# Retention queries and keys as a seven-product scheme per head, and a new order of the products around it

## Chip, cores and metric

The kernel runs on one core of one Trainium2 chip. The metric is the device time of one execution in microseconds (us). Three executions of the kernel before took 1118.16, 1119.35 and 1121.62 us; the median is 1119.35 us.

## The reference, cut to what matters

One layer of a decoder: a retention branch and a latent attention branch read the same normalised input, each is projected and gated, and an MLP and a gated embedding follow. The sequence has 512 tokens, the model 1024 channels. The change is in the retention branch, which has 4 heads with 256 channels for queries and keys and 512 for values:

```python
proj = h @ w_in                       # h: 512 x 1024, normalised
rq, rk, rv, rg, cq, ckv, krope, gr, gm = jnp.split(proj, offsets, axis=-1)
rq = rope(rq.reshape(B, S, RET_HEADS, RET_QK_DIM), pos)
rk = rope(rk.reshape(B, S, RET_HEADS, RET_QK_DIM), pos) * (RET_QK_DIM ** -0.5)
ro = retention(rq, rk, rv)            # scores q k^T with a decay, times v
ro = rms_norm(ro, ret_norm...)
a_ret = (ro * jax.nn.silu(rg)) @ w_br
...
def rope(x, pos):                     # x1, x2: the two halves of 256
    return jnp.concatenate([x1 * cos - x2 * sin, x2 * cos + x1 * sin], axis=-1)
```

## The kernel before, in words

Every large product is made with split operands: a float32 number is held as a high and a low part (tiles that end in h and l, weights `wh_` and `wl_`), and `mm3` issues three matmuls for one pair of 128-row tiles: low by high, high by low, high by high. A weight tile of 512 KB (128 x 1024) is loaded raw (`wr_`), ScalarE rounds it to `wh_` (line 260), and VectorE subtracts to get `wl_` (line 264, or line 266 where the sign is turned). There are 6 raw buffers and NW=3 buffers each for the high and low parts, which all weights use in turn.

The program is a list of steps, `step(key, function, ...)`. `run_steps` walks through it, splits the next step's weights AHEAD=1 step early, and starts the raw loads of weights with an "sw" key up to PREP=3 steps early. The final order of the instructions on each engine is set by the framework's scheduler from these steps; each engine then takes its own instructions strictly in that order.

**Products in seven.** The values `rv` and the gates `rg` of two heads at a time, and the MLP's `dn`, are already made by a scheme of seven products instead of eight (Strassen-Winograd): operands are sums and differences of blocks, seven block products are formed, and four output blocks are combined from them. `CHAIN` says which products share one set of PSUM sums: 1, 6, 5, 3 accumulate in set a, 7 and 4 in set c, 2 alone in b. In between, `seven_out` reads the running sums out. The x operands (`XS[p]`) are made by `x_operand`; the weight operands are made by the DMA: `prepare` loads a block by SyncE's queue and adds others to it in the same buffer by accumulating loads on GpSimd's queue (POOL). A new raw tile is loaded for products 1, 7, 2, 5 and 3; 7 and 5 get a further block added at once, and products 6 and 4 are made by adding one more block to the tile of 7, once that tile has been split for the product before. The products come in the order 1, 7, 2, 6, 4, 5, 3. One product of `rv` or `rg` is 24 matmuls of 128x512.

**Queries and keys.** Each head has four projections, `rq` and `rk` with n=0 and n=1 (`ret_qk`), each 8 x 3 = 24 matmuls of 128x512. VectorE multiplies the sums by cos and sin (lines 809, 810), combines the two halves (lines 815, 816) and splits the result into `rqx`, `rqy`, `rkx`, `rky` (lines 305, 306).

**The rest of a head.** `ret_scores` (sums `rs`), `ret_attend` (sums `ro`, result `o`), `ret_gated` (`o` times the gate, line 851), `ret_turned` (transposes `ot` on TensorE), `branch_r` (four steps of 24 matmuls, sums `br`). The step list interleaves these with projections of the next head, so that TensorE has other work while VectorE finishes. After the heads come three `gr` gate steps (n = 5, 6, 7), between them the last `ret_turned`, then the last branch steps. In the attention phase before, `scores(h, blocks)` (sums `sc`) and `head_factor` (which ends with a small matmul `pbk`) alternate, and `fill` places steps of the gate projection `gm` into gaps.

Of the kernel before, what the change touches and what calls it, by code (L numbers as in the profile page):

```python
# [51 lines left out]

C_ID, C_MASK, C_IND, C_INVR, C_INVM, C_SGN, C_N = 0, 128, 256, 260, 261, 262, 263

NDYN, NKEEP, NW, NRAW, NDRAW, AHEAD, PREP, EARLY, PAD = 45, 16, 3, 6, 4, 1, 3, 5, 104
GROUPS = DFF // 1024


# [8 lines left out]
def _rng(a, n):  # L67
    return np.arange(a, a + n)


def chunk_specs():

    spec = {}

    def add(key, name, rows, cols):
        spec[key] = (len(rows) // P * len(cols), lambda w: _tiles(w[name], rows, cols))

    half = ROPE // 2
    cat = np.concatenate
    kr = cat([_rng(O_KR, half), _rng(O_KR + half, half), _rng(O_KR + half, half), _rng(O_KR, half)])  # L80
    first = cat([_rng(O_CKV, KVL), kr])
    full = _rng(0, D)
    for k in range(8):
        add(("a1", k), "w_in", _rng(k * P, P), first)
    for n in range(3):
        add(("cq", n), "w_in", full, _rng(O_CQ + n * P, P))
    for h in range(MH):
        spec["kq", h] = (2 * P + 3 * P, lambda w, h=h: cat([
            _tiles(w["w_ukv"], _rng(0, KVL), _rng(h * 256, P)), _tiles(w["w_uq"], _rng(0, QL), _rng(h * QKD, P))], axis=1))
    for p in range(4):  # L90
        add(("v", p), "w_ukv", _rng(0, KVL), cat([_rng(h * 256 + P, P) for h in (2 * p, 2 * p + 1)]))
    for gq in range(2):
        ac = cat([_rng((4 * gq + i) * QKD + NOPE, half) for i in range(4)])
        add(("qr", gq), "w_uq", _rng(0, QL), cat([ac, ac + half]))
    for n in range(8):
        for k in range(2):
            add(("gm", n, k), "w_in", _rng(k * S, S), _rng(O_GM + n * P, P))
            if n < EARLY:
                add(("gr", n, k), "w_in", _rng(k * S, S), _rng(O_GR + n * P, P))
        if n >= EARLY:  # L100
            add(("gr", n), "w_in", full, _rng(O_GR + n * P, P))
        for key, name in (("bm", "w_bm"), ("o", "w_o"), ("pg", "w_ple_gate")):
            add((key, n), name, full, _rng(n * P, P))
    for h in range(RH):
        for key, o in (("rq", O_RQ), ("rk", O_RK)):
            for n in range(2):
                add((key, h, n), "w_in", full, _rng(o + h * RQK + n * P, P))
        for k in range(4):
            add(("br", h, k), "w_br", _rng(h * RV, RV), _rng(2 * k * P, 2 * P))

    for kb in range(2):
        for fb in range(2):
            for q in range(RH // 2):
                for c in range(2):
# [32 lines left out]
def trunk_layer(ctx: ExitStack, tc: tile.TileContext, xT, pT, pos, gains, const, decay, wstream, outT):  # L147
# [314 lines left out]


    def trig(name, posf, inv):
        ang, kf, c_, s_ = T(name + "a"), T(name + "k"), T(name + "c"), T(name + "s")
# [686 lines left out]
    for h in range(MH):  # L1152
        p, more = h // 2, h + 2 < MH
        if h % 2 == 0 and h:
            step(None, scores, h, (0, 1))
            step(None, head_factor, h)
            step(None, scores, h, (2, 3))
            step(None, head_factor, h + 1)
        else:
            step(None, scores, h)  # L1160
# [49 lines left out]
            step(None, x_operand, 7)  # L1210
    for p in (1, 2, 4):
        step(None, x_operand, p)
    def qk(h, key, n):
        step((key, h, n), ret_qk, h, key, n)

    def branch(h, *ks):
        for k in ks if h >= 0 else ():
            step(("br", h, k), branch_r, h, k)

    for q in range(RH // 2):  # L1220
        h = 2 * q
# [8 lines left out]
        for kind in ("rv", "rg"):  # L1230
            for p in (1, 7, 2, 6, 4, 5, 3):
                for c in range(2):
                    step(("sw", (kind, q), p, c), ret_seven, kind, q, p, c)
                if (kind, q) == ("rv", 0) and p in (1, 7, 2):
                    step(None, x_operand, {1: 6, 7: 5, 2: 3}[p])
                if (kind, p) == ("rv", 1):
                    branch(h - 1, 2)
                    step(None, ret_scores, h)
                    branch(h - 1, 3)
                if (kind, p) == ("rg", 1):  # L1240
                    step(None, ret_attend, h)
                if (kind, p) == ("rg", 4):
                    step(None, ret_gated, h)
        qk(h + 1, "rq", 0)
# [132 lines left out]
```

## Time and profile before

| What | Value |
|---|---|
| median of 3 executions | 1119.35 us |
| the profiled execution, its own time | 1118.9 us |
| its span | 1117.1 us |
| TensorE (PE) busy | 1098.4 us, 98%, 5137 matmuls |
| weight loads (PEld) | 909.6 us, beside PE |
| VectorE (DVE) busy | 711.4 us, 64% |
| ScalarE (ACT) busy | 541.1 us, 48% |
| GpSimd (POOL) busy | 90.4 us, 8% |
| DMA | 178.02 MB; mean 159 GB/s |

A busy share is an average over the whole span. The releaser behind an arrow ("<-DVE wl_rg L266") is the instruction whose end let the waiting one start. Matmuls are pipelined: their shown durations overlap, so the cost of one is read from the distance between two starts.

### The profile page before, as it was taken

Reading aid. Unit: us, or ns where it says so; the run is one execution under the profiler, and the core shown is the slowest. Engines: PE = TensorE matmul, PEld = TensorE weight load, DVE = VectorE, ACT = ScalarE, POOL = GpSimd, SP = SyncE. Lnnn points to the kernel's source line nnn. Section 1 sums busy time; section 2 is a strip of 40 time slices with the busy share of each in tenths; the row PEclk is TensorE's granted clock in tenths of the full one; section 3 lists DMA queues with packets and bytes.
Section 4 is the critical chain, followed back from the end, with each engine's and each line's share of the span. In section 5 each row is a group of like instructions: output and inputs, shape, how many; then the busy total and the mean of one; then the engine's idle time right before and its main releaser. Section 6 shows DMA issues by size and latency. Waiting matters only on the chain.

```text
span 1117.1 us, 13841 instructions
## 1 busy us (share of the span) xinstructions
PE 1098.4 (98%) x5137; PEld 909.6 (81%) x5137; DVE 711.4 (64%) x1135; ACT 541.1 (48%) x785; POOL 90.4 (8%) x121
## 2 busy tenths in 40 slices
PE   9999999999999999999999999999999999999998
PEld 7877878888878788887878877788888888888887
DVE  7697677566774655646456467555466666668785
ACT  7637556453465635345554644434444443444552
POOL 0000000001102001031100100010100100101000
PEclk9999999999999999999999999999999999999999
DMA  7242231466779734488873934693855765737511
GB/s 263 63 136 76 64 104 57 141 208 220 185 189 241 196 124 169 108 195 209 205 212 96 281 121 145 197 265 116 178 161 166 177 168 152 185 129 195 163 57 57
DMA packets 59860, 178.02 MB, mean 159 GB/s; under 512 B 7376, under 2 KB 8784, under 8 KB 59536
## 3 DMA queue, kind: packets, MB, share of 16 engines
q1 hardware_dynamic: 45168, 129.66, 35.1%
q0 software_dynamic: 14480, 47.46, 21.7%
q8 instruction: 40, 0.66, 0.2%
q14 instruction: 28, 0.23, 0.1%
q10 hardware_dynamic: 144, 0.03, 0.0%
HBM read 157.97 MB, written 17.04 MB: 157 GB/s over the span
## 4 chain that ended last, share of the span: by engine, by line
PE 75%; DMA 9%; DVE 6%; issue 5%; ACT 2%; POOL 1%; SPq 0%; POOLq 0%; ACTq 0%; DVEq 0%
PE up L167 16%; PE dn L167 14%; PE br L167 5%; DMA wr_rg<-wstream 5%; PE pg L167 4%; PE bm L167 4%; PE wo L167 4%; PE gr L167 3%; PE rq L167 3%; PE rk L167 3%; PE gm L167 3%; PE rg L167 2%; DMA wr_rv<-wstream 2%; PE sc L167 2%; PE rv L167 2%
## 5 line engine op out<-in xcount | busy, mean ns | idle before, releaser
L167 PE MATMUL dn<-wh_dn,cl 128*128 128x512 f32 x224 | 87.2, 389 | 0.0
L167 PE MATMUL dn<-wh_dn,ch 128*128 128x512 f32 x224 | 87.1, 389 | 0.0
L167 PE MATMUL dn<-wl_dn,ch 128*128 128x512 f32 x224 | 87.1, 389 | 0.0
L260 ACT ACTIVATE wh_dn<-wr_dn 128x1024 fp32r<-128x1024 f32 x32 | 34.0, 1062 | 74.5 <-PE up L167 54.3
L260 ACT ACTIVATE wh_up<-wr_up 128x1024 fp32r<-128x1024 f32 x32 | 34.0, 1061 | 58.8 <-PE up L167 29.3
L264 DVE TENSOR_TENSOR wl_dn<-wr_dn,wh_dn 128x1024 fp32r<-128x1024 f32 x32 | 39.1, 1221 | 25.8 <-ACT wh_dn L260 25.8
L264 DVE TENSOR_TENSOR wl_up<-wr_up,wh_up 128x1024 fp32r<-128x1024 f32 x32 | 39.1, 1223 | 18.8 <-ACT wh_up L260 18.8
L167 PEld LDWEIGHTS dn<-wl_dn,ch 128*128 128x128 f32 x224 | 42.0, 188 | 8.8
L167 PEld LDWEIGHTS dn<-wh_dn,cl 128*128 128x128 f32 x224 | 42.0, 188 | 8.7
L167 PEld LDWEIGHTS dn<-wh_dn,ch 128*128 128x128 f32 x224 | 42.0, 188 | 8.6
L982 DVE SCALAR_TENSOR_TENSOR f<-up,bcx 128x512 f32<-128x512 f32 x32 | 20.6, 686 | 44.4 <-PE up L167 44.4
L260 ACT ACTIVATE wh_dn<-dr_dn 128x1024 fp32r<-128x1024 f32 x24 | 25.4, 1060 | 44.3 <-PE up L167 29.4
L264 DVE TENSOR_TENSOR wl_dn<-dr_dn,wh_dn 128x1024 fp32r<-128x1024 f32 x24 | 29.4, 1223 | 24.5 <-ACT wh_dn L260 24.5
L222 POOL DMA_DIRECT2D dr_dn<-wstream x24 | 21.1, 892 | 294.0 <-DVE wl_dn L264 107.5
L260 ACT ACTIVATE wh_rg<-wr_rg 128x1024 fp32r<-128x1024 f32 x28 | 29.4, 1059 | 30.6 <-DMA wr_rg<-wstream 15.5
L260 ACT ACTIVATE wh_rv<-wr_rv 128x1024 fp32r<-128x1024 f32 x28 | 29.4, 1059 | 29.7 <-DMA wr_rv<-wstream 7.2
L264 DVE TENSOR_TENSOR wl_rg<-wr_rg,wh_rg 128x1024 fp32r<-128x1024 f32 x20 | 24.3, 1224 | 20.6 <-ACT wh_rg L260 20.4
L264 DVE TENSOR_TENSOR wl_rv<-wr_rv,wh_rv 128x1024 fp32r<-128x1024 f32 x20 | 24.3, 1223 | 14.0 <-ACT wh_rv L260 14.0
L1040 DVE TENSOR_TENSOR d<-d,dn 128x1024 f32<-128x1024 f32 x24 | 29.3, 1219 | 6.0 <-PE dn L167 6.0
L264 DVE TENSOR_TENSOR wl_br<-wr_br,wh_br 128x1024 fp32r<-128x1024 f32 x16 | 19.5, 1220 | 21.2 <-ACT wh_br L260 21.2
L260 ACT ACTIVATE wh_br<-wr_br 128x1024 fp32r<-128x1024 f32 x16 | 16.9, 1059 | 31.7 <-PE rk L167 16.3
L871 ACT ACTIVATE rt<-br 128x512 f32<-128x512 f32 x24 | 13.9, 594 | 25.5 <-PE br L167 25.5
(1819 smaller groups left out, 3449.2 us busy)
## 6 DMA issues: line engine op xcount, KB each, us to landing
wr_up<-wstream SPq DMA_DIRECT2D x32, 512.0 KB, 4.1
wr_dn<-wstream SPq DMA_DIRECT2D x32, 512.0 KB, 3.5
dr_dn<-wstream POOLq DMA_DIRECT2D x24, 512.0 KB, 7.0
wr_rv<-wstream SPq DMA_DIRECT2D x20, 512.0 KB, 4.2
wr_rg<-wstream SPq DMA_DIRECT2D x20, 512.0 KB, 4.8
wr_rv<-wstream POOLq DMA_DIRECT2D x16, 512.0 KB, 7.1
wr_rg<-wstream POOLq DMA_DIRECT2D x16, 512.0 KB, 7.9
wr_br<-wstream SPq DMA_DIRECT2D x16, 512.0 KB, 3.6
```

Source lines behind the costliest of these rows:

```text
L167: return tc.keep_in_program_order(nc.tensor.matmul(*a, **k))
L222: nc.gpsimd.dma_start(raw, chunk(("w", blk, kb, fb, c)), accum_op=ALU.add)
L260: i = ACT(hi, raw, AF.Copy, scale=sign)
L264: TT(lo, raw, hi.bitcast(F32), op=ALU.subtract)
L871: ACT(t, ps, AF.Copy)
L982: STT(u[:, i], ps[:, i], 0.0, V["bcx2"], op0=ALU.max, op1=ALU.mult)
L1040: TT(to, to, dps[p], op=ALU.add if sign > 0 else ALU.subtract)
```

## The change

Each head's four projections become one product in seven. Queries are one output half and keys the other; with the input halves and the token halves this gives a two-by-two block form. One of its products has 4 x 2 x 3 = 24 matmuls of 128x256 (stationary: 128 columns of the weights; moving: 256 tokens of `XS[p]`, which the `rv` and `rg` products use too), so a head has 168 of them. The results come as blocks of 256 tokens; they are multiplied by a table `tab` (cos, sin, cos, with one more ScalarE copy) and combined in 256-column pieces. The keys are now "sw" keys, so their weights are loaded by `prepare`.

The order of all sevens changes from 1, 7, 2, 6, 4, 5, 3 to 1, 7, 2, 6, 5, 4, 3, so that product 4 (set c) stands between 5 and 3, which share set a. Products of a head's queries and keys are placed among others: those of head 0 between products of `rv`, products 1 and 7 of an odd head between `rg` 6 and 5, its product 2 after `rg` 3. Smaller moves: two `fill` steps of `gm` before `rotary_key` and one after (before: one and two), score blocks 0, 1, 2 ahead of `head_factor` (before: 0, 1), and the last `ret_turned` after the `gr` step 6 (before: after 5).

```diff
-NDYN, NKEEP, NW, NRAW, NDRAW, AHEAD, PREP, EARLY, PAD = 45, 16, 3, 6, 4, 1, 3, 5, 104
+NDYN, NKEEP, NW, NRAW, NDRAW, AHEAD, PREP, EARLY, PAD = 42, 16, 3, 6, 4, 1, 3, 5, 104
...
+            for h in range(RH):
+                add(("w", ("qk", h), kb, fb, 0), "w_in", _rng(kb * S, S), _rng((O_RQ, O_RK)[fb] + h * RQK, RQK))
...
-    def ret_qk(w, h, key, n):
-        d = R[h]
-        ps = proj(B(f"{key}{h}{n}"), xn, w)
-        a, b = T(f"{key}a{h}{n}"), T(f"{key}b{h}{n}")
-        TT(a, ps, V["cr"] if n == 0 else V["sr"], op=ALU.mult)
-        TT(b, ps, V["sr"] if n == 0 else V["cr"], op=ALU.mult)
-        if n == 0:
-            d[key] = (a, b)
-        else:
-            a0, b0 = d[key]
-            TT(a0, a0, a, op=ALU.subtract)
-            TT(b0, b0, b, op=ALU.add)
-            d[key] = (split(a0, f"{key}x{h}"), split(b0, f"{key}y{h}"))
+    def ret_qk(w, h, p):
+        ch, d = CHAIN[p], R[h]
+        if p in (1, 7, 2):
+            qkps[ch] = B(f"qk{h}{p}")
+        ps = qkps[ch]
+        for o in range(2):
+            for k in range(4):
+                mm3(ps[:, o * 256:o * 256 + 256], cut(w, k * 256 + o * P), XS[p][k], p in (1, 7, 2) and o + k == 0,
+                    o == 1 and k == 3, skip_group_check=True)
+        done = seven_out(d.setdefault("qk", {}), p, ps, f"qk{h}_")
+        if not done:
+            return
+        blk, t = done
+        key, cs = ("rq", "rk")[blk % 10 - 1], slice(256 * (blk // 10 - 1), 256 * (blk // 10))
+        a, b = T(f"{key}a{h}{blk}"), T(f"{key}b{h}{blk}")
+        TT(two(a), two(t), V["tab"][:, 0:2, cs], op=ALU.mult)
+        TT(two(b), two(t), V["tab"][:, 1:3, cs], op=ALU.mult)
+        first = key not in d
+        if first:
+            d[key] = (T(f"{key}u{h}"), T(f"{key}v{h}"))
+        u, v = d[key]
+        TT(u[:, cs], a[:, 0:256], a[:, 256:512], op=ALU.subtract)
+        TT(v[:, cs], b[:, 0:256], b[:, 256:512], op=ALU.add)
+        if not first:
+            d[key] = (split(u, f"{key}x{h}"), split(v, f"{key}y{h}"))
...
+    fill(2)
+    step(None, rotary_key)
     fill(1)
-    step(None, rotary_key)
-    fill(2)
...
-            step(None, scores, h, (0, 1))
+            step(None, scores, h, (0, 1, 2))
             step(None, head_factor, h)
-            step(None, scores, h, (2, 3))
+            step(None, scores, h, (3,))
...
         if q:
+            qk(h, 1, 7, 2)
             step(None, ret_turned, h - 1)
-        qk(h, "rq", 1)
-        branch(h - 1, 0)
-        qk(h, "rk", 0)
-        branch(h - 1, 1)
-        qk(h, "rk", 1)
...
+            qk(h, 6)
+            branch(h - 1, 0)
+            qk(h, 5, 4, 3)
+            branch(h - 1, 1)
+            seven("rv", q, 1)
+            branch(h - 1, 2)
+            step(None, ret_scores, h)
+            seven("rv", q, 7, 2, 6)
+            branch(h - 1, 3)
+        else:
+            step(None, x_operand, 6)
+            qk(h, 1, 7)
+            step(None, x_operand, 5)
+            qk(h, 2)
+            seven("rv", q, 1)
+            step(None, x_operand, 3)
+            qk(h, 6)
+            seven("rv", q, 7)
+            qk(h, 5)
+            seven("rv", q, 2)
+            qk(h, 4, 3)
+            seven("rv", q, 6)
+            step(None, ret_scores, h)
+        seven("rv", q, 5, 4, 3)
+        seven("rg", q, 1)
+        step(None, ret_attend, h)
+        seven("rg", q, 7, 2, 6)
+        qk(h + 1, 1, 7)
+        seven("rg", q, 5, 4)
+        step(None, ret_gated, h)
+        seven("rg", q, 3)
+        qk(h + 1, 2)
         step(None, ret_turned, h)
+        qk(h + 1, 6)
         branch(h, 0)
+        qk(h + 1, 5, 4, 3)
         branch(h, 1)
         step(None, ret_scores, h + 1)
...
-        if n == EARLY:
+        if n == EARLY + 1:
             step(None, ret_turned, RH - 1)
```

How the rows move is shown at two places. In the rows, `<-` stands between what an instruction writes and what it reads; `rs` are the sums of the scores, `s` the scores times the decay.

**The scores of head 1, VectorE and ScalarE.** The scores' first matmul reads the low part `rkx1l`. Before, VectorE:

```order
L815 TENSOR_TENSOR rka_4019<-rka_4019,rka_4094 128x512
L816 TENSOR_TENSOR rkb_4020<-rkb_4020,rkb_4095 128x512
L264 TENSOR_TENSOR wl_br_3_4217<-wr_br_3_4214,wh_br_3_4216 128x1024
L306 TENSOR_TENSOR rkx1l<-rka_4019,rkx1h 128x512
L306 TENSOR_TENSOR rky1l<-rkb_4020,rky1h 128x512
L830 TENSOR_TENSOR s_4157<-rs_4150,dec_4148 128x512
L264 TENSOR_TENSOR wl_rq_0_4257<-wr_rq_0_4254,wh_rq_0_4256 128x1024
```

Of the change, VectorE and then ScalarE (`wr_qk_4432` is the weight tile of product 1 of head 2's queries and keys):

```order
L831 TENSOR_TENSOR rka_4306<-qk_3867,tab 128x512
L832 TENSOR_TENSOR rkb_4307<-qk_3867,tab 128x512
L837 TENSOR_TENSOR rku_4229<-rka_4306 128x256
L838 TENSOR_TENSOR rkv_4230<-rkb_4307 128x256
L265 SCALAR_TENSOR_TENSOR wl_qk_4472<-wr_qk_4432,wh_qk_4471 128x1024
L305 TENSOR_TENSOR rkx1l<-rku_4229,rkx1h 128x512
L305 TENSOR_TENSOR rky1l<-rkv_4230,rky1h 128x512
L853 TENSOR_TENSOR s_4369<-rs_4362,dec_4360 128x512
```

```order
L259 ACTIVATE wh_br_3_4428<-wr_br_3_4426 128x1024
L304 ACTIVATE rqx1h<-rqu_4080 128x512
L304 ACTIVATE rqy1h<-rqv_4081 128x512
L259 ACTIVATE wh_qk_4471<-wr_qk_4432 128x1024
L304 ACTIVATE rkx1h<-rku_4229 128x512
L304 ACTIVATE rky1h<-rkv_4230 128x512
```

The weights that the program needs next stood behind `rkx1h` and `rkx1l` before; in the change those of head 2's first product stand ahead of both. With three buffers, `wh_qk_4471` goes into the one of the second branch step's weights. At head 3 the rows are the same with the `gr` weights of n = 5 in that place.

**The scores of head 0, VectorE.** Before, where each `rk` projection's sums come 5 rows ahead of the next:

```order
L809 TENSOR_TENSOR rka_3119<-rk_3094,trs 128x512
L810 TENSOR_TENSOR rkb_3120<-rk_3094,trc 128x512
L815 TENSOR_TENSOR rka_3083<-rka_3083,rka_3119 128x512
L816 TENSOR_TENSOR rkb_3084<-rkb_3084,rkb_3120 128x512
L264 TENSOR_TENSOR wl_rv_3155<-wr_rv_3091,wh_rv_3154 128x1024
L306 TENSOR_TENSOR rkx0l<-rka_3083,rkx0h 128x512
```

Of the change, from behind the sum that product 4 completes (`qk_21_3191`, with a weight split after it):

```order
L831 TENSOR_TENSOR rqa_3350<-qk_21_3191,tab 128x512
L832 TENSOR_TENSOR rqb_3351<-qk_21_3191,tab 128x512
L837 TENSOR_TENSOR rqu_3100<-rqa_3350 128x256
L838 TENSOR_TENSOR rqv_3101<-rqb_3351 128x256
L263 TENSOR_TENSOR wl_rv_3429<-wr_rv_3368,wh_rv_3428 128x1024
L305 TENSOR_TENSOR rqx0l<-rqu_3100,rqx0h 128x512
L305 TENSOR_TENSOR rqy0l<-rqv_3101,rqy0h 128x512
L831 TENSOR_TENSOR rka_3395<-qk_2991,tab 128x512
L832 TENSOR_TENSOR rkb_3396<-qk_2991,tab 128x512
L837 TENSOR_TENSOR rku_3269<-rka_3395 128x256
L838 TENSOR_TENSOR rkv_3270<-rkb_3396 128x256
L263 TENSOR_TENSOR wl_rv_3496<-wr_rv_3413,wh_rv_3495 128x1024
```

Directly behind the last of them stands `rkx0l`, then the weights `wl_rv_3513` and `rky0l`. Queries and keys of the second token half are finished right before the scores, where before only the second half of the keys was.

## Rows read from the trace of the kernel before

**Rows 1.** The page: busy times; DMA queues (packets, MB, share of 16 engines).

```profile
PE 1098.4 (98%) x5137; PEld 909.6 (81%) x5137; DVE 711.4 (64%) x1135; ACT 541.1 (48%) x785; POOL 90.4 (8%) x121
...
q1 hardware_dynamic: 45168, 129.66, 35.1%
q0 software_dynamic: 14480, 47.46, 21.7%
```

**Rows 2.** Timeline, PE: first matmuls of rq and of rk (48 apart).

```profile
275.44 0.39 PE L167 MATMUL rq<-xn0h,wl_rq 128*128 128x512 f32 x1
286.32 0.39 PE L167 MATMUL rk<-xn0h,wl_rk 128*128 128x512 f32 x1
```

**Rows 3.** Timeline, PE: the same form with 256 columns (first and last of 41).

```profile
1107.56 0.28 PE L167 MATMUL pg<-x3g2l,wh_pg 128*128 128x256 f32 x1
...
1112.36 0.28 PE L167 MATMUL pg<-x3g7h,wh_pg 128*128 128x256 f32 x1
```

**Rows 4.** Groups by line, PE, 270 to 660 us: matmuls that waited (busy, mean ns | idle before).

```profile
L167 PE MATMUL rg<-wl_rg,xn4h 128*128 128x512 f32 x8 | 3.4, 419 | 0.9 <-DVE wl_rg L266 0.9
L167 PE MATMUL rv<-wh_rv,s30l 128*128 128x512 f32 x8 | 3.3, 414 | 0.9 <-DVE cv L754 0.9
L167 PE MATMUL rg<-wh_rg,s30l 128*128 128x512 f32 x8 | 3.3, 410 | 0.9 <-DVE z L754 0.9
...
L167 PE MATMUL rg<-wl_rg,xn6h 128*128 128x512 f32 x8 | 3.2, 404 | 0.8 <-DVE wl_rg L266 0.8
L167 PE MATMUL rv<-wl_rv,xn6h 128*128 128x512 f32 x8 | 3.2, 402 | 0.5 <-DVE wl_rv L266 0.5
```

**Rows 5.** Timeline, PE: the last transposes, and those of head 1.

```profile
641.75 0.39 PE L167 MATMUL gr<-xn7h,wh_gr 128*128 128x512 f32 x1
...
644.97 1.20 PE L167 MATMUL ot<-cst,o 128*128 128x128 f32 x9 [0.34 <-DVE o L851]
...
450.48 0.81 PE L167 MATMUL ot<-cst,o 128*128 128x128 f32 x3
451.62 0.55 PE L167 MATMUL ot<-cst,o 128*128 128x128 f32 x3 [0.33 <-DVE o L851]
```

**Rows 6.** Timeline, PE: two waits of the attention phase.

```profile
68.77 0.47 PE L167 MATMUL gm<-xg0h,wl_gm 128*128 128x512 f32 x1 [1.55 <-DVE wl_gm L264]
...
161.21 0.65 PE L167 MATMUL pbk<-cst,hr 128*128 128x128 f32 x4 [1.00 <-DVE hr L602]
```

**Rows 7.** Timeline around the scores of head 1: PE, DVE and ACT.

```profile
417.81 0.39 PE L167 MATMUL rk<-xn7h,wh_rk 128*128 128x512 f32 x1
418.23 0.69 DVE L809 TENSOR_TENSOR rka<-rk,trs 128x512 f32<-128x512 f32 x1 [2.63 <-PE rk L167]
418.84 0.68 DVE L810 TENSOR_TENSOR rkb<-rk,trc 128x512 f32<-128x512 f32 x1
420.64 1.22 DVE L264 TENSOR_TENSOR wl_br<-wr_br,wh_br 128x1024 fp32r<-128x1024 f32 x1
421.77 0.68 DVE L306 TENSOR_TENSOR rkx1l<-rka,rkx1h 128x512 fp32r<-128x512 f32 x1
...
418.23 1.06 ACT L260 ACTIVATE wh_br<-wr_br 128x1024 fp32r<-128x1024 f32 x1 [3.89 <-PE rk L167]
```

**Rows 8.** Timeline, DVE: four operations on 256 columns, one group.

```profile
311.93 1.43 DVE L733 TENSOR_TENSOR sy<-xr,xr 128x256 f32<-128x256 f32 x4
```

**Rows 9.** DMA issues, 270 to 650 us: KB each, median us to landing.

```profile
wr_rg<-wstream POOLq DMA_DIRECT2D x16, 512.0 KB, 7.9
```

**Rows 10.** Stretches: span, busy of PE, PEld, DVE, ACT, POOL, granted clock, DMA share, GB/s.

```profile
270.00:650.00 380.00, 373.58 (x1689) 307.20 (x1688) 222.39 (x325) 191.57 (x286) 52.40 (x67) 1.00 0.70 185
...
1112.00:1114.00 2.00, 0.64 (x6) 0.43 (x4) 0.84 (x2) 0.42 (x1) 0.00 (x0) 1.00 0.19 66
1114.00:1116.00 2.00, 0.00 (x0) 0.00 (x0) 0.43 (x2) 0.00 (x0) 0.00 (x0) 0.74 0.19 66
```

**Rows 11.** Timeline, PE: the first matmuls of the program.

```profile
1.46 4.21 PE L167 MATMUL zero<-zero 128*128 128x512 f32 x9 [1.46 <-DVE zero L360]
```

More of the change, by code (lines that the diff above doesn't have):

```diff
@@ L104, in chunk_specs @@
     for h in range(RH):
-        for key, o in (("rq", O_RQ), ("rk", O_RK)):
-            for n in range(2):
-                add((key, h, n), "w_in", full, _rng(o + h * RQK + n * P, P))
         for k in range(4):
@@ L464, in trig @@
     def trig(name, posf, inv):
-        ang, kf, c_, s_ = T(name + "a"), T(name + "k"), T(name + "c"), T(name + "s")
+        ang, kf = T(name + "a"), T(name + "k")
+        if name == "tr":
+            V["tab"] = dyn.tile([P, 3, S], F32, tag="tab", name="tab", bufs=1)
+            c_, s_ = V["tab"][:, 0], V["tab"][:, 1]
+        else:
+            c_, s_ = T(name + "c"), T(name + "s")
         TS(ang, posf, inv, None, op0=ALU.mult)
@@ L503, in ret_sincos @@
     def ret_sincos():
-        V["cr"], V["sr"] = sincos(*V["ar"])
+        sincos(*V["ar"])
+        ACT(V["tab"][:, 2], V["tab"][:, 0], AF.Copy)
     def rotary_key():
@@ L747, in seven_out @@
             to = {1: 11, 7: 22, 6: 21}[p]
-            c[to] = (T if to == 21 or name[0] == "c" else Z)(f"{name}{to}")
+            c[to] = (Z if to != 21 and name[0] == "z" else T)(f"{name}{to}")
             ACT(c[to], ps, AF.Copy, scale=1.0 if p == 7 else -1.0)
@@ L803, in odd_v, with two @@
             R[h]["v"][j] = split(src, f"rv{h}{j}", lo=lo)
-    def ret_qk(w, h, key, n):
-        d = R[h]
-        ps = proj(B(f"{key}{h}{n}"), xn, w)
-        a, b = T(f"{key}a{h}{n}"), T(f"{key}b{h}{n}")
-        TT(a, ps, V["cr"] if n == 0 else V["sr"], op=ALU.mult)
-        TT(b, ps, V["sr"] if n == 0 else V["cr"], op=ALU.mult)
-        if n == 0:
-            d[key] = (a, b)
-        else:
-            a0, b0 = d[key]
-            TT(a0, a0, a, op=ALU.subtract)
-            TT(b0, b0, b, op=ALU.add)
-            d[key] = (split(a0, f"{key}x{h}"), split(b0, f"{key}y{h}"))
+    qkps = {}
+    def two(t):
+        return t.rearrange("p (k c) -> p k c", k=2)
+    def ret_qk(w, h, p):
[23 more added lines that the diff above has]
+            d[key] = (split(u, f"{key}x{h}"), split(v, f"{key}y{h}"))
     def ret_scores(h):
@@ L1212, in trunk_layer, with qk, seven @@
         step(None, x_operand, p)
-    def qk(h, key, n):
-        step((key, h, n), ret_qk, h, key, n)
+    def qk(h, *ps):
+        for p in ps:
+            step(("sw", ("qk", h), p, 0), ret_qk, h, p)
+    def seven(kind, q, *ps):
+        for p in ps:
+            for c in range(2):
+                step(("sw", (kind, q), p, c), ret_seven, kind, q, p, c)
     def branch(h, *ks):
@@ L1221, in trunk_layer @@
         h = 2 * q
-        qk(h, "rq", 0)
         if q:
+            qk(h, 1, 7, 2)
             step(None, ret_turned, h - 1)
-        qk(h, "rq", 1)
-        branch(h - 1, 0)
-        qk(h, "rk", 0)
-        branch(h - 1, 1)
-        qk(h, "rk", 1)
[L1230 to L1244, printed above, removed]
+            qk(h, 6)
[7 more added lines that the diff above has]
+            branch(h - 1, 3)
+        else:
+            step(None, x_operand, 6)
[20 more added lines that the diff above has]
+        qk(h + 1, 2)
         step(None, ret_turned, h)
-        qk(h + 1, "rq", 1)
-        qk(h + 1, "rk", 0)
+        qk(h + 1, 6)
         branch(h, 0)
-        qk(h + 1, "rk", 1)
+        qk(h + 1, 5, 4, 3)
         branch(h, 1)
```

## The prediction, made before the changed kernel was run

> **What bounds the kernel now.** I read the page first: TensorE (PE) is busy 98% of the span, VectorE (DVE) 64%, ScalarE (ACT) 48% [rows 1]. So the time is the sum of the matmuls plus the pauses between them, and the change can pay in two ways only: fewer or cheaper matmuls, or fewer pauses. The timeline gives the price of a matmul from start to start, the groups by line show which matmuls waited and for whom, the stretches give clock and DMA load. In 270 to 650 us, where the change lies, PE has 373.58 us of work in 380.00 at a granted clock of 1.00, beside a DMA share of 0.70 [rows 10]. Idle DVE and ACT there are cover for what the change adds to them, as long as no matmul waits for its result.
>
> The sum is made against the profiled execution, 1118.9 us; the median of the runs shown is 1119.35 us, 0.45 us above it, far inside their spread. A measurement of this kernel can tell about 0.3% from no change, 3.4 us: below about 1116.0 is faster, above 1122.7 slower.
>
> **Fewer columns.** 48 matmuls of 512 columns take 286.32 - 275.44 = 10.88 us, 0.2267 us each [rows 2]; a head's 96 take 21.76 us. With 256 columns, 40 distances from 1107.56 to 1112.36 make 0.120 us each [rows 3]; a head's 168 take 20.16 us. Gain 1.60 us a head, **6.4 us** for four. The new form is that of rows 3 (128 weight columns stationary, 256 tokens moving), so I take its price as it is. One rule speaks against this: the Trainium skill ("TensorE: Matmul & The Clock Gate", section "Back-to-back issue gap") gives sustained 81 ns for 128 columns and 131 ns for 512; halfway in columns that makes, as my estimate from the page, 98 ns for 256, and by it a head would lose 168 x 98 - 96 x 131 ns = 3.9 us, the kernel 15.6. The trace agrees with neither figure: 226.7 ns for 512 and 120 ns for 256, and the measurement decides.
>
> **The new order of all sevens.** Product 4 waits for weights that are still being added up in the tile of 7, and product 3 for the read-out of set a behind product 5. Idle before them is 0.9 + 0.9 + 0.9 + 0.8 + 0.5 = 4.0 us [rows 4], nine waits by the timeline. A shown matmul lasts 0.39 us where the next would start after 0.23, so each wait costs 0.16 us more than its idle time: 4.0 + 1.4 = **5.4 us**. With 5 ahead of 4, 4 has 24 matmuls (5.44 us) more for waits of under 1 us, and with 4 ahead of 3, set a has 5.44 us to be read. I count all of it; the bounds are 0 and 5.4.
>
> **Smaller moves.** The last transposes: from 641.75 to 644.97 us where one matmul and three transposes (0.11 us each, nine in 1.20) would take 0.56, so 2.66 us [rows 5]; a `gr` step of 5.44 us is put in between, gain **2.7 us**. Head 1's transposes: 1.14 us instead of 0.33 [rows 5], now with product 6, 2 or later work ahead, **0.8 us**. `pbk` waits 1.00 us [rows 6] and gets one more score block ahead, **1.0 us**. The `gm` weights come 1.55 us late [rows 6]; in the new order one DVE operation of 0.6 us less stands ahead, **0.6 us**. Gains together 16.9 us. The table's extra copy and the new `fill` order lie beside PE work.
>
> **New waits.** The engines are in-order. A DVE operation costs from start to start 0.61 us on 512 columns, 1.13 on 1024 [rows 7], and (1.43 - 0.42) / 3 = 0.34 on 256 [rows 8]; it starts 0.19 us after the sums it needs (417.81 + 0.23 to 418.23), and ACT rounds a weight tile in 1.06 [rows 7].
> - Head 1's scores. ACT now has `wh_qk` of head 2 ahead of `rkx1h`, and DVE `wl_qk` ahead of `rkx1l`. The buffer of `wh_qk` is free only when the second branch step ends, and the scores follow that step directly. So PE stands: 0.19 + 1.06 + 0.08 + 1.13 + 0.69 and 0.1 to PE, **3.2 us**.
> - Head 3's scores: the same with the `gr` weights, **3.2 us**. Head 2's have a product of `rv` and a branch step between and are covered.
> - Head 0's scores. From the sum of product 4 to `rkx0l` DVE has eight operations on 512 columns, four on 256 and three on 1024: 4.9 + 1.4 + 3.4 = 9.7 us, with 0.19 of lag and an estimated operation left over (0.6) 10.5. PE has product 3 (2.88) and an `rv` product (5.44), 8.3. A wait of 2.1 us or a little more; then `wl_rv` and `rky0l` (1.73) against three matmuls (0.68), 1.0 more: **3.1 us**.
> - The first `rv` product's second half. Behind head 0's product 2 DVE has a sum, two splits and two multiplications (5 x 0.61), two pieces of 256 (0.68) and the weights (1.22), 5.1 us with lag, against 2.72 of PE work and 0.23: **2.2 us**.
>
> Together 11.7 us. Each lies between nothing (if DVE and ACT reach that place earlier than I assume) and its chain at full durations, some 10% more: 0 to 13 us.
>
> **DMA.** A head's four loads of 512 KB become five on SyncE's queue and four accumulating ones on POOL's. By the queues of rows 1 the first kind takes 35.1% of 1117.1 us x 0.524 / 129.66 = 1.6 us of all engines, the second 21.7% x 1117.1 x 0.524 / 47.46 = 2.7; so 12.3 us a head, 49 in all, and the share in the stage rises from 0.70 to some 0.83. Accumulating loads land in 7.9 us [rows 9]. The tightest users: product 4 of heads 1, 2, 3 starts 2.88 + 5.44 + 2.88 = 11.2 us after product 6, whose split frees the tile; 7.9 and a split of 2.3 make 10.2. Product 6 of head 2 is about as tight. Nothing in the trace shows this load; bounds are 0 and a wait like the worst of rows 4 (0.9 + 0.16) at all four, 4 us. I take **0.7 us**, since 1 us is left at the median landing.
>
> **Sum:** 1118.9 - 6.4 - 5.4 - 2.7 - 0.8 - 1.0 - 0.6 + 11.7 + 0.7 = **1114.4 us**.
>
> **Rivals.**
> - *The new waits are covered.* DVE and ACT are far from full, and three of the four waits rest on a few operations of backlog. Without any: 1114.4 - 11.7 = 1102.7 us; with half, 1108.5. Against it stands the in-order place of `wh_qk` and its buffer, which no faster engine moves. Chance 0.20.
> - *Accumulating loads come late: slower.* The four tight products wait once landings pass 8.9 us; at 12 us each waits some 3 us, 12 us in all: 1114.4 - 0.7 + 12 = 1125.7. It makes the kernel slower from about 2.2 us a product (4 x 2.2 = 8.8 against the 8.6 from 1114.4 - 0.7 up to 1122.3). For it: the higher share, and product 4's waits in rows 4. Against it: the median landing. Chance 0.12.
> - *The clock falls in the two pauses of 3.2 us.* At the end of the program, behind the last matmul at 1112.36 [rows 3], the granted clock is 1.00 up to 1114 and 0.74 in the next two us [rows 10]; at the start, at 1.2 GHz, nine matmuls took 4.21 us [rows 11] instead of 9 x 0.227 = 2.04. Twice 2.2 us gives 1118.8: no change. The Trainium skill (the same page, section "Why this matters for your kernels") warns of idle gaps between bursts of matmuls; pauses of up to 1.55 us here left the clock at 1.00 [rows 6, 10]. Chance 0.08.
> - *The new order doesn't do what it is for:* loads and read-outs are late by the same amount, since more traffic stands ahead. Without its 5.4 us: 1119.8, no change. Chance 0.06.
> - *Weight loads bound the 256-column matmuls.* They take 909.6 / 5137 = 0.177 us each [rows 1]; 168 x 0.177 = 29.7 us a head instead of 20.2 would make 1152.6. Rows 3 have as many loads per matmul and run at 0.120. Chance 0.02.
>
> **How the numbers follow.** My forecast has 0.52, its own range 1109.5 to 1118 by the bounds of the new waits and of the DMA: 0.40 of it faster, 0.12 within 0.3%. Faster: 0.40 + 0.20 = 0.60. The same: 0.12, the clock 0.07, the order 0.05, late loads 0.02, together 0.26. Slower: late loads 0.10, clock and order 0.01 each, weight loads 0.02, together 0.14. The range reaches to 1103.0, leaving out some 0.06 of the covered case, and to 1121.0, leaving out late and bound loads, some 0.12.
>
> **What would show it.** Starts of `qk` matmuls 0.120 us apart; no idle before products 4 and 3 of `rv` and `rg`, none over 0.3 us before the last `ot` or `pbk`; idle of about 3 us before the first `rs` matmul of heads 1 and 3, released by `rkx1l` and `rkx3l`, 2 to 3 before that of head 0, and 2 in the first `rv` product; none before head 2's. Idle before `qk` products 4 or 6 with a weight load behind it means late loads; a granted clock under 1.00 in the stretch of a pause means the clock. The prediction is wrong if `rs` starts without a wait, or if a pause stands at a place not named here.

## The result, and the profile after

The changed kernel took 1124.24 us (median of 9 executions, 1122.7 to 1125.97) beside 1119.35 us before: a ratio of 1.0042, 95% interval 1.0031 to 1.0053. By the ratio it is slower by 4.7 us, where 1114.4 was forecast with a range of 1103 to 1121. The profiled execution took 1124.27 us, its span is 1122.5.

The page's first part of the changed kernel (answers to [rows 1]):

```profile
PE 1096.4 (98%) x5425; PEld 925.9 (82%) x5425; DVE 734.4 (65%) x1175; ACT 562.7 (50%) x812; POOL 104.1 (9%) x137
```

PE has less work than before, 1096.4 against 1098.4 us, in a longer span. A matmul at half clock is shown longer (0.63 instead of 0.39 us, below), so part of the gain is hidden even in the busy time.

**What came as the prediction said.** The timeline, PE, the first matmuls of three `qk` products, 24 apart (answers to [rows 2, 3]):

```profile
281.10 0.28 PE L166 MATMUL qk<-xn0h,wl_qk 128*128 128x256 f32 x1
283.98 0.28 PE L166 MATMUL qk<-s70h,wl_qk 128*128 128x256 f32 x1
286.86 0.28 PE L166 MATMUL qk<-xn4h,wl_qk 128*128 128x256 f32 x1
```

2.88 us for 24, 0.120 us each. The groups by line, PE, 270 to 660 us (answers to [rows 4, 5]):

```profile
L166 PE MATMUL rv<-wl_rv,xn6h 128*128 128x512 f32 x8 | 3.1, 389 | 0.0
L166 PE MATMUL rv<-wh_rv,s30l 128*128 128x512 f32 x8 | 3.1, 389 | 0.0
...
L166 PE MATMUL rg<-wl_rg,xn4h 128*128 128x512 f32 x8 | 3.1, 389 | 0.0
...
L166 PE MATMUL rg<-wh_rg,s30l 128*128 128x512 f32 x8 | 3.1, 389 | 0.0
L166 PE MATMUL ot<-cst,o 128*128 128x128 f32 x64 | 7.6, 273 | 0.0
```

No product 4, no product 3 and no transpose waits any more in this stretch, and `pbk` no longer waits in the attention phase. The DMA share in 270 to 650 us rose from 0.70 to 0.82, where 0.83 was forecast. The new waits stand where they were forecast. The scores of head 1, from the timeline (answers to [rows 7]):

```profile
427.43 0.39 PE L166 MATMUL br<-rog03h,wh_br 128*128 128x512 f32 x1
427.90 1.06 ACT L259 ACTIVATE wh_qk<-wr_qk 128x1024 fp32r<-128x1024 f32 x1 [3.00 <-issue]
428.99 1.23 DVE L265 SCALAR_TENSOR_TENSOR wl_qk<-wr_qk,wh_qk 128x1024 fp32r<-128x1024 f32 x1 [0.73 <-ACT wh_qk L259]
430.13 0.69 DVE L305 TENSOR_TENSOR rkx1l<-rku,rkx1h 128x512 fp32r<-128x512 f32 x1
430.88 0.80 PE L166 MATMUL rs<-rqx1h,rkx1l 128*128 128x512 f32 x1 [3.06 <-DVE rkx1l L305]
431.47 0.63 PE L166 MATMUL rs<-rqx1l,rkx1h 128*128 128x512 f32 x1
431.90 0.63 PE L166 MATMUL rs<-rqx1h,rkx1h 128*128 128x512 f32 x1
```

The chain is the forecast one, step by step: the branch step ends, ACT rounds head 2's weights, DVE splits them, then comes `rkx1l`. From 427.43 to 430.88 are 3.45 us; less one matmul of 0.23 that is 3.22.

**What did not.** The last two rows are 0.43 us apart, at the lower of the clock's two levels (1.2 instead of 2.4 GHz); the prediction had them at 0.227. And two long pauses stand in the attention phase, where the prediction counted nothing. From the timeline, DVE, ACT and PE:

```profile
71.82 0.69 DVE L305 TENSOR_TENSOR qr20l<-o,qr20h 128x512 fp32r<-128x512 f32 x1 [2.16 <-PE sqr L166]
...
75.69 0.74 ACT L259 ACTIVATE wh_kq<-wr_kq 128x640 fp32r<-128x640 f32 x1 [4.10 <-PE gm L166]
76.61 0.68 DVE L518 TENSOR_TENSOR krot<-t,prho 64x512 f32<-64x512 f32 x1
77.33 0.63 ACT L304 ACTIVATE kph<-krot 128x512 fp32r<-128x512 f32 x1 [0.90 <-DVE krot L518]
77.86 0.58 ACT L592 ACTIVATE sums<-sums 128x512 f32<-128x512 f32 x1
78.50 0.66 PE L166 MATMUL st<-cst,sums 128*128 128x128 f32 x4 [2.84 <-ACT sums L592]
...
94.79 1.28 ACT L489 ACT_TABLE_LOAD   x1
97.26 1.28 ACT L653 ACT_TABLE_LOAD   x1
102.93 0.89 PE L166 MATMUL pt0a<-cst,p 128*128 128x128 f32 x4 [2.61 <-DVE p L656]
```

The first looks like the pause above, since on ACT a weight split that waits for PE (`wh_kq`, behind a `gm` step) now stands ahead of what PE needs next. But the split is not what ends last: behind it ACT still waits 0.90 us for `krot` from DVE, and `sums` stands behind `kph`, as it did before. DVE is late because `qr20l` waits 2.16 us for PE's `sqr` matmuls. It reads only `o` and `qr20h`, which were done before, so by elimination the wait is for the buffer that it writes. Before, it started without a wait. The second ends with the softmax `p`, between whose exponentials the sine table's activations and two more activation-table loads have moved. Before, the same transposes waited 0.68 us and the scores behind them 0.82:

```profile
68.54 0.68 DVE L306 TENSOR_TENSOR qr20l<-o,qr20h 128x512 fp32r<-128x512 f32 x1
...
97.24 0.66 PE L167 MATMUL pt0a<-cst,p 128*128 128x128 f32 x4 [0.68 <-DVE p L651]
100.80 0.44 PE L167 MATMUL sc<-k1h,q1l 128*128 128x384 f32 x1 [0.82 <-ACT sqk L525]
```

The stretches of the changed kernel in which the granted clock falls (columns as in [rows 10]):

```profile
70.00:80.00 10.00, 7.16 (x41) 5.07 (x40) 7.97 (x17) 2.48 (x4) 0.92 (x2) 0.97 0.41 113
80.00:90.00 10.00, 10.00 (x51) 8.67 (x50) 6.78 (x25) 2.34 (x4) 0.72 (x2) 0.86 0.76 253
...
100.00:110.00 10.00, 7.39 (x44) 6.28 (x42) 7.79 (x20) 8.41 (x18) 0.00 (x0) 0.83 0.15 54
320.00:330.00 10.00, 7.28 (x29) 5.37 (x28) 8.95 (x14) 6.24 (x9) 0.55 (x1) 0.92 1.01 261
330.00:340.00 10.00, 10.00 (x49) 8.77 (x48) 6.05 (x11) 3.74 (x6) 1.05 (x2) 0.90 0.46 99
...
430.00:440.00 10.00, 9.12 (x40) 7.94 (x41) 5.85 (x12) 3.54 (x7) 2.76 (x5) 0.83 0.77 228
...
620.00:630.00 10.00, 7.59 (x34) 6.64 (x35) 6.60 (x12) 5.61 (x12) 1.73 (x2) 0.83 0.72 185
```

Each holds a pause named above, at the scores of head 0, 1 or 3 or in the attention phase, or follows it: five falls, one behind each pause (at head 0, behind two short ones).

### The profile page after: what moved, and what is told of

Its sections match the earlier page's. It is cut to its first block, busy times and chain, and to the rows that moved or that the text cites. A ratio compares the mean times of both kernels' runs of the same rounds, so it can differ in the third digit from the quotient of the medians.

```text
span 1122.5 us, 14539 instructions
## 1 busy us (share of the span) xinstructions
PE 1096.4 (98%) x5425; PEld 925.9 (82%) x5425; DVE 734.4 (65%) x1175; ACT 562.7 (50%) x812; POOL 104.1 (9%) x137
## 4 chain that ended last, share of the span: by engine, by line
PE 88%; DVE 6%; ACT 2%; issue 2%; DMA 1%; POOL 0%; DVEq 0%; ACTq 0%
PE up L166 16%; PE dn L166 14%; PE rg L166 7%; PE rv L166 6%; PE br L166 5%; PE qk L166 5%; PE pg L166 4%; PE gr L166 4%; PE bm L166 4%; PE wo L166 4%; PE gm L166 3%; PE sc L166 2%; PE ro L166 2%; PE rs L166 2%; PE pA L166 2%
## 5 line engine op out<-in xcount | busy, mean ns | idle before, releaser
L259 ACT ACTIVATE wh_qk<-wr_qk 128x1024 fp32r<-128x1024 f32 x28 | 29.7, 1062 | 33.0 <-PE br L166 6.9
L263 DVE TENSOR_TENSOR wl_qk<-wr_qk,wh_qk 128x1024 fp32r<-128x1024 f32 x20 | 24.4, 1222 | 23.7 <-ACT wh_qk L259 23.6
```

Source lines behind the costliest of these rows:

```text
L259: i = ACT(hi, raw, AF.Copy, scale=sign)
L263: TT(lo, raw, hi.bitcast(F32), op=ALU.subtract)
```

## Experiments

All times stand beside runs of the kernel before on the same chip, 1117.88 to 1118.42 us in the four groups.

**e1, the new order alone.**

```diff
-            for p in (1, 7, 2, 6, 4, 5, 3):
+            for p in (1, 7, 2, 6, 5, 4, 3):
```

> The kernel before with one edit: the rv and rg products in the order 1, 7, 2, 6, 5, 4, 3. If the step of the prediction holds, the waits ahead of products 4 and 3 (5.4 us by the rows) go and nothing takes their place: about 1114 us. Rival: the loads and read-outs are late by the same amount, about 1119 us.

1112.01 us, ratio 0.9943 (0.9926 to 0.9960). The one-line part of the change is worth 6.3 us by the ratio (4.5 to 8.3 by its interval), where 5.4 was forecast. Not all of it is products 4 and 3: in this profile two waits of `rg` are left, 1.1 us together, and the transposes `ot` wait 0.7 us in all instead of 2.2.

**e2, the buffers alone**, in the kernel before:

```diff
-NDYN, NKEEP, NW, NRAW, NDRAW, AHEAD, PREP, EARLY, PAD = 45, 16, 3, 6, 4, 1, 3, 5, 104
+NDYN, NKEEP, NW, NRAW, NDRAW, AHEAD, PREP, EARLY, PAD = 42, 16, 3, 6, 4, 1, 3, 5, 104
```

> The kernel before with 42 instead of 45 general buffers and nothing else. Theory: the three buffers that make room for the table move a weight split ahead of the rotary key on ScalarE, so the pause of about 3 us before the st matmul near 75 us is here too, with the lower clock behind it: 3 to 4 us slower than before, 1122 to 1124 us. Rival: the pause comes from the moved fill steps, and this kernel takes 1119 us with no pause over 1 us there.

1122.41 us, ratio 1.0043 (1.0025 to 1.0062), 4.8 us slower by the ratio. Timeline, DVE, ACT and PE:

```profile
72.91 0.69 DVE L306 TENSOR_TENSOR qr20l<-o,qr20h 128x512 fp32r<-128x512 f32 x1 [2.16 <-PE sqr L167]
...
76.77 0.74 ACT L260 ACTIVATE wh_kq<-wr_kq 128x640 fp32r<-128x640 f32 x1 [4.10 <-PE gm L167]
77.81 0.63 ACT L305 ACTIVATE kph<-krot 128x512 fp32r<-128x512 f32 x1 [0.30 <-DVE krot L513]
...
78.98 0.66 PE L167 MATMUL st<-cst,sums 128*128 128x128 f32 x4 [2.25 <-ACT sums L587]
...
280.70 0.39 PE L167 MATMUL rq<-xn0h,wl_rq 128*128 128x512 f32 x1
```

Same wait of DVE for `sqr`, same order on ACT and a pause of the same form, without any other part of the change: the smaller number of buffers is enough for it, far from the code that the change is about. The second pause isn't here: the transposes wait 0.65 us, as before. The clock was 1.00 in this execution, so the part expected from a lower clock did not come, and the pause is not the whole cost: the retention part starts at 280.70 us, 5.26 later than before [rows 2]. Another 1.0 us of that is a wait of a `gm` step for `mx`, 1.6 us instead of 0.6; the rest was not taken apart.

**e3, the table by copies.**

```diff
-        sincos(*V["ar"])
-        ACT(V["tab"][:, 2], V["tab"][:, 0], AF.Copy)
+        c, s = sincos(*V["ar"])
+        V["tab"] = dyn.tile([P, 3, S], F32, tag="tab", name="tab", bufs=1)
+        for i, t in enumerate((c, s, c)):
+            ACT(V["tab"][:, i], t, AF.Copy)
```

> The changed kernel, but cos and sin are made in two tiles as before and copied into the table. Theory: the sine activations then stand ahead of the softmax on ScalarE, the two added activation-table loads go, and so does the pause of 2.8 us before the transposes of p near 100 us: about 3 us less than the changed kernel, 1121 us. Rival: the pause stays and the two further copies add to it, 1124 us or more.

1124.59 us, ratio 1.0057 (1.0040 to 1.0075): nothing gained. Timeline, PE:

```profile
95.36 0.50 PE L166 MATMUL pk<-ckv0h,wl_kq 128*128 128x512 f32 x1 [0.68 <-ACT kf L613]
103.01 0.66 PE L166 MATMUL pt0a<-cst,p 128*128 128x128 f32 x4 [1.24 <-DVE p L653]
106.56 0.44 PE L166 MATMUL sc<-k1h,q1l 128*128 128x384 f32 x1 [0.82 <-ACT sqk L527]
```

The pause is cut into three that come to as much (2.74 us). The two added table loads are gone here (one is left, at 97.95 us) and the wait is not, so they are not the cause by themselves. What is, these runs don't show.

**e4, matmuls in the pauses of heads 1 and 3.** In `ret_scores`, before the first `mm3` of an odd head:

```diff
+            for _ in range(12 if h % 2 and j == 0 else 0):
+                MM(ps, d["rq"][0][0][:, 0:P], d["rq"][0][0], start=True, stop=True)
```

> The changed kernel with 12 matmuls of 512 columns, whose results are overwritten, ahead of the scores of heads 1 and 3 (2.7 us of work in pauses of 3.2). Theory: the pauses themselves stay, but the matmuls behind them run at 0.227 us instead of 0.427, which gives back 1.6 us at each place, 3.2 in all: 1121 us, granted clock 1.00 at both places. Rival: the slow matmuls behind a pause have another cause (loads, PSUM), the clock stays low, 1124 us.

1123.14 us, ratio 1.0041 (1.0025 to 1.0056): a miss, in four executions not told apart from the change where 3.2 us were expected. Its own profiled one, 1121.69 us, has a granted clock of 1.00 at both places, as the theory had it, but falls elsewhere come and go by execution. So the changed kernel was run again (**e9**), and beside it a version that fills all five pauses (**e10**).

> The changed kernel itself, beside the next one on the same chip: about 1.004 times the kernel before.

1122.74 us, ratio 1.0041 (1.0027 to 1.0056). Timeline, PE, the scores of head 1 in this execution:

```profile
430.68 0.50 PE L166 MATMUL rs<-rqx1h,rkx1l 128*128 128x512 f32 x1 [3.06 <-DVE rkx1l L305]
431.02 0.40 PE L166 MATMUL rs<-rqx1l,rkx1h 128*128 128x512 f32 x1
431.26 0.39 PE L166 MATMUL rs<-rqx1h,rkx1h 128*128 128x512 f32 x1
```

The same kernel, the same pause of 3.06 us, and the matmuls behind it run 0.24 us apart: this time the clock stayed.

```diff
+    def busy(ps, n, x):
+        for _ in range(n):
+            MM(ps, x[0][0][:, 0:P], x[0][0], start=True, stop=True)
...
+        if p == 0:
+            busy(ps, 11, xg)
...
+            if h == 0 and nm == "a":
+                busy(ps, 10, xg)
...
+            if j == 0 and h != 2:
+                busy(ps, 12 if h else 8, xn)
```

> The changed kernel with 8 to 12 extra matmuls of 512 columns, whose results are overwritten, in each of its five long pauses (st near 75 us, transposes near 100, scores of heads 0, 1 and 3), each a little shorter than the pause. Theory: what ends each pause is DVE or ACT, so the pauses keep their length, but the clock stays at 1.00 and the matmuls behind run at full speed: 5 to 7 us less than the changed kernel. Rival: the extra matmuls delay what follows as much as the clock gives back, no difference.

1118.28 us, ratio 0.9994 (0.9982 to 1.0006), 4.5 us below the changed kernel beside it. Stretches:

```profile
100.00:110.00 10.00, 8.82 (x59) 6.79 (x58) 8.34 (x22) 8.32 (x19) 0.00 (x0) 1.00 0.20 54
...
430.00:440.00 10.00, 10.00 (x52) 8.61 (x51) 5.33 (x11) 4.73 (x8) 0.58 (x2) 1.00 0.51 178
...
620.00:630.00 10.00, 10.00 (x52) 8.57 (x51) 6.53 (x13) 7.23 (x12) 1.70 (x2) 1.00 1.08 297
```

Fifty-three matmuls of no use make the kernel faster. What ends the pauses is as late as before; the clock behind them is 1.00. From the first matmul of head 1's scores to the first of the branch step behind them it is 3.98 us here (427.92 to 431.90) and 5.53 in the changed kernel (430.88 to 436.41): that fall cost 1.55 us. With the clock up, the change neither gains nor loses.

**e5, a branch step ahead of the odd heads' scores.**

```diff
+        branch(h, 2)
         step(None, ret_scores, h + 1)
         step(None, odd_v, h + 1)
-        branch(h, 2, 3)
+        branch(h, 3)
```

> The changed kernel with the third branch step ahead of the scores of heads 1 and 3 instead of behind them (24 matmuls, 5.44 us of cover). Theory: both pauses of 3.2 us and the slow matmuls behind them (1.6 us each) go: 9.6 us less, about 1114.5 us. Rival: the weights of the step after it are late in turn and PE waits there, gain under 3 us.

1119.79 us, ratio 1.0008 (0.9992 to 1.0023): about 4 us gained by the ratios, under half of the 9.6 expected. At head 3 PE no longer waits. At head 1 the pause moved to where its values, loaded only behind the scores, are first used:

```profile
446.57 0.50 PE L166 MATMUL ro<-rv10h,atl 128*128 128x512 f32 x1 [2.43 <-ACT rv10h L304]
```

The chain behind it goes through the load of `rv10l` on GpSimd's queue.

**e6, head 0.** `x_operand` 5 and 3 come one step later, and the scores behind `rv` 5:

```diff
-            seven("rv", q, 6)
+            seven("rv", q, 6, 5)
             step(None, ret_scores, h)
-        seven("rv", q, 5, 4, 3)
+        seven("rv", q, *((5, 4, 3) if q else (4, 3)))
```

> The changed kernel with head 0 reordered: the x operands of products 5 and 3 one step later, the scores behind product 5 of rv instead of 6. Theory: the waits of 1.9 us in the first rv product and of 2.1 + 0.9 us at the scores, and the slow matmuls behind the latter, go: about 5 us less, 1119 us. Rival: the operands of 5 and 3 are then late and the waits move there: 1123 us or more.

1122.99 us, ratio 1.0044 (1.0025 to 1.0063): no gain. The wait in the first `rv` product is gone, that at the scores became a longer one:

```profile
328.13 0.50 PE L166 MATMUL rv<-wh_rv,s50l 128*128 128x512 f32 x1 [4.49 <-ACT cv L754]
```

In the new order 5 follows 6 on the same sums. The scores had stood between them as cover for ACT's read-out, which queues behind the splits of `rkx` and `rky`.

**e7, more fill.** EARLY = 6 gives two more `fill` steps; they go ahead of `st` and of the first transposes.

```diff
     step(None, pair_sums, 0)
-    fill(1)
+    fill(2)
...
             if h == 0:
-                fill(1)
+                fill(2)
```

> The changed kernel with one more gate (gr 5) made in the attention phase, its two halves as a second fill step ahead of the st matmul near 75 us and of the transposes of p near 100 us (2.72 us of matmuls each, the same number in all). Theory: the pauses of 3.0 and 2.8 us and the slow matmuls behind them go for the most part: 6 to 7.5 us less, about 1117.5 us. Rival: ScalarE, not PE, sets the end of this phase, and the time comes back later in it: gain under 2 us.

1117.82 us, ratio 0.9991 (0.9981 to 1.0001): some 5.5 us below the change, a little under the 6 to 7.5 expected. In the profiled execution no wait over 0.3 us is left at either place.

**e8, all three together**, and `branch(h - 1, 0)` of head 2 behind product 5:

> The three edits before together, and head 1's first branch step one product later (a wait of 1.4 us at rog10l). If the parts add up: 1124.2 - 9.6 - 5 - 7 - 1.4 = 1101 us, faster than both kernels. Rival: what is freed shows a next wait in each place, and half of it is left: 1112 us.

1110.8 us, ratio 0.9930 (0.9909 to 0.9950): faster than both kernels, but 10 us above the sum of parts. The pauses of e6 and e5 are in it (3.68 and 1.04 us here), and the step moved for `rog10l` put product 5 of head 2 directly behind 6 (1.63 us, released by the read-out on ACT); the rest was not taken apart.

**e11 and e12, two more orders.** Beside e7's fill and the later x operands of e6, e11 has:

```diff
-            qk(h, 5)
+            qk(h, 5, 4)
             seven("rv", q, 2)
-            qk(h, 4, 3)
+            qk(h, 3)
...
-        step(None, ret_scores, h + 1)
         step(None, odd_v, h + 1)
-        branch(h, 2, 3)
+        branch(h, 2)
+        step(None, ret_scores, h + 1)
+        branch(h, 3)
...
-        if n == EARLY + 1:
+        if n == EARLY:
```

and e12 also, in head 2:

```diff
             qk(h, 6)
+            seven("rv", q, 1)
             branch(h - 1, 0)
             qk(h, 5, 4, 3)
             branch(h - 1, 1)
-            seven("rv", q, 1)
             branch(h - 1, 2)
```

> The change with the extra fill steps of e7, head 0's product 4 ahead of rv 2 and product 3 behind it, head 1's and 3's values loaded and third branch step ahead of their scores, the last transposes behind the first of two gr steps. Theory: with the pause at product 5 of rv (3.8 us), that at the ro matmuls of head 1 (2.3) and that of the last branch (1.8) gone, 1102 to 1104 us. Rival: a wait of similar length stands elsewhere, 1110 us as e8.

1112.92 us, ratio 0.9957 (0.9938 to 0.9976): a miss, some 9 us above what was expected. With head 1's values loaded ahead of a branch step, the pause at `ro` is longer than in e5:

```profile
440.74 0.79 PE L166 MATMUL ro<-rv10h,atl 128*128 128x512 f32 x1 [4.35 <-DVE atl L305]
```

The chain that ends there shows why. The splits of the values stand ahead of `s` and `atl` on ACT and DVE, and they wait for loads on GpSimd's queue (start, us):

```profile
430.35 5.84 DMA rv12l<-v2d
```

> As e11, and in heads 2 the first rv product ahead of the first branch step of head 1. Theory: the wait of 1.4 us for rog10l goes as well: 1.4 us less than e11. Rival: the scores of head 2 lose their cover and wait as long.

1120.35 us, ratio 1.0013 (1.0002 to 1.0023): a miss. It differs from e11 in head 2 only, yet its profiled execution has the same `ro` pause 3.2 us longer. The same chain there:

```profile
434.08 7.94 DMA rv12l<-v2d
...
442.57 1.05 ACT wh_qk L259
```

The load takes 2.1 us more, and a weight split now stands on ACT between the splits of `rv12` and `rv13`: together the 3.2 us. Why the load took longer, and the rest of the 7.4 us between e11 and e12, stay open.

**e13, cover kept.** Built from what the misses showed: nothing that shares sums stands back to back, and the scores get the next head's first product as cover, whose weights had blocked them. The core of the edit, beside that of e7 (head 2 then starts with product 7, and the x operands 5 and 3 come later as in e6):

```diff
-            qk(h, 5)
-            seven("rv", q, 2)
-            qk(h, 4, 3)
-            seven("rv", q, 6)
+            qk(h, 5, 4)
+            seven("rv", q, 2, 6)
+            qk(h, 3)
+            seven("rv", q, 5)
             step(None, ret_scores, h)
...
         branch(h, 1)
+        if q:
+            branch(h, 2)
+        else:
+            qk(h + 2, 1)
         step(None, ret_scores, h + 1)
...
```

> The change with the extra fill steps of e7; head 0's products 5 and 4 together, rv 6 ahead of product 3 and the scores behind rv 5; head 2's first product (2.88 us) ahead of head 1's scores, whose other steps stay as in the change; head 3's third branch step ahead of its scores. If the sevens of queries and keys are worth their 6.4 us and only pauses hid it, this is about e1 less 6 to 8 us, 1103 to 1105 us on e1's chip. Rival: with the pauses gone the added loads or VectorE's work hold PE up elsewhere, and it stays near 1110.

1102.57 us, ratio 0.9864 (0.9846 to 0.9882): 15 us faster than before, 20 than the change, some 9 below e1 by the ratios. The page's first part and two stretches:

```profile
PE 1089.3 (99%) x5425; PEld 919.0 (83%) x5425; DVE 734.5 (67%) x1177; ACT 560.2 (51%) x811; POOL 105.1 (10%) x138
```

```profile
320.00:330.00 10.00, 8.55 (x43) 7.00 (x42) 8.02 (x12) 5.05 (x7) 0.44 (x1) 1.00 0.92 293
420.00:430.00 10.00, 9.72 (x62) 8.81 (x61) 8.08 (x15) 6.27 (x11) 4.30 (x8) 1.00 0.79 201
```

The matmuls are those of the change in number and kind; only their order differs, and PE's busy time falls by 7.1 us, with no stretch under 1.00 ahead of the program's end. At a DMA share of 0.92 no matmul waits for a load; the longest wait left in the retention part is 1.4 us, for DVE's `rky0l` at head 0's scores.

**e14**, as e13, with head 1's transposes one product earlier:

```diff
-            qk(h, 7, 2)
+            qk(h, 7)
             step(None, ret_turned, h - 1)
-            qk(h, 6)
+            qk(h, 2, 6)
```

> As e13, with the transposes of head 1 ahead of head 2's product 2. Theory: the wait of 1.4 us for rog10l goes, and the transposes wait less than 0.5 for o: about 1 us less than e13. Rival: o is late by as much, no difference.

1106.44 us, ratio 0.9893 (0.9875 to 0.9911), 3.9 us slower than e13: the rival, and more. In e13's profile the branch step had no wait for `rog10l` left to lose. Here the transposes wait in four places, 2.6 us together; the three after this one, of 0.27, 0.34 and 0.34 us, are put down to DVE's `o`:

```profile
449.58 0.30 PE L166 MATMUL ot<-cst,o 128*128 128x128 f32 x1 [1.66 <-ACT wh_br L259]
```

## Why the prediction was wrong

- **Fewer columns, 6.4 us: right.** The price of 0.120 us was taken from another product of the same form, and it held. By the estimate from the sustained figures of the Trainium skill ("TensorE: Matmul & The Clock Gate", section "Back-to-back issue gap"; 98 ns against 131) the change would lose; rows with 0.120 against 0.227 say otherwise. (256 columns are a third of the way from 128 to 512, not half; 98 is right for a third.) e13, below e1 by some 9 us with these products and the fill of e7, fits a gain that is kept once the pauses are gone; how the 9 divide was not taken apart.
- **New order, 5.4 us: right** in the changed kernel, where no product 4 or 3 waits; 6.3 measured alone (e1), with some of that in the transposes.
- **Last transposes and head 1's: right** where they stood; 1.1 us came back behind head 1's, at the branch step that reads `rog10l` and `rog11l` (0.75 + 0.35). `pbk` gave its 1.0; the `gm` weights still come 1.10 us late instead of 1.55, a gain of 0.45 and not 0.6.
- **New waits, 11.7 us: right in place, cause and size.** Forecast 3.2, 3.2, 2.1 + 1.0 and 2.2; idle before the first matmul 3.06, 3.06, 1.95 + 0.77 and 1.76, each some 0.2 more from start to start.
- **DMA, 0.7 us: nothing.** Product 4 and 6 of `qk` never waited for their weights in the changed kernel; the accumulating loads of `qk` landed in 6.1 us, where 7.9 was taken. In 320 to 330 us, at a share of 1.01, PE's waits are those of head 0's scores, released by DVE. The rival of late loads had the right side for a wrong reason. Loads on GpSimd's queue did hold PE up in e5, e11 and e12, those of head 1's values.
- **The step that failed:** "The table's extra copy and the new `fill` order lie beside PE work". It cost 4.0 us: idle of 2.84 + 2.61 us where 0.68 + 0.82 stood. In e10, where the clock stays up, the retention part starts at 279.42 us, 3.98 later than before [rows 2]. What it missed: NDYN falls from 45 to 42 to make room for the table, and with it DVE waits for PE ahead of `qr20l` and the scheduler's order changes in a phase where the diff seems to move only small steps (e2). The prediction read the new order in the retention part alone. Only the pause at `st` is shown to come from the buffers. The cause of the second, at the transposes, stays open: the buffers alone leave it as it was (e2), and moving the sines away only divided it (e3). That more PE work covers both is shown (e7).
- **The second: the clock rival had 0.08 and decided.** With every pause filled the kernel is 4.5 us faster (e10), inside the stated range. The forecast priced a fall at 2.2 us and took two places; it happens at up to five, at 1.55 us where it was measured, and the attention pauses, not seen, were among them. The price came from the program's first matmuls, where the profile's clock column shows 1.00: a row of slow matmuls, not of a granted clock. The Trainium skill's warning of idle gaps between bursts ("TensorE: Matmul & The Clock Gate", section "Why this matters for your kernels") agrees with e10, where filled gaps left the clock at 1.00. The same gap can also cost nothing in another execution (e9).

Put together, 1114.4 + 4.0 + 4.5 + 1.1 = 1124.0 us, against 1124.27 measured in the profile. That it closes so well is in part luck: the 0.7 us for DMA is still in it, e1 gave 0.9 more than the new order's 5.4, and the 4.5 come from runs on another chip.

## What to carry to other kernels

When PE is full, price a change by its pauses, and read the order of every engine from the first instruction to the last where a scheduler sets it: a smaller pool alone made VectorE wait 2.16 us in the attention phase, 200 us ahead of the part that the change is about. Look there for an instruction that waits though all it reads is done: it may be waiting for its buffer. A weight split whose buffer comes free with the step that runs now must not stand ahead of what the next step needs; give that next step the product those weights belong to as cover. Pauses like these on PE, of two to three microseconds, cost their length and here about a third of it again in slow matmuls (4.5 us for 14.3 us of pauses, e10).

## What the hardware showed that was not expected

The clock's fall behind a pause is not a fixed matter of its length: the pause of 3.06 us at head 1 was followed by matmuls 0.43 us apart in one execution and 0.24 in another of the same kernel, the fall at head 0 came behind two shorter pauses (1.95 and 0.77 us, three matmuls between them), and behind e2's pause of 2.25 us there was none. Over nine executions of the changed kernel the mean granted clock and the time go together: 0.990 with 1125.5 to 1126.0 us, 0.993 with 1122.7 to 1123.3, about 1 us for each 0.001. With all pauses filled (e10) the twelve executions lie within 1.6 us, at 0.999 or 1.000.
